# Output projection with four whole token blocks, three MLP pairs multiplied ahead, and the attention sink as a score column

## The chip, the cores and the metric

The kernel runs on one core of a Trainium2 chip. Its engines are TensorE (PE, with its weight loads as PEld), VectorE (DVE), ScalarE (ACT), GpSimd (POOL) and SyncE (SP), which issues the DMA transfers. The metric is the device time of one launch in microseconds (us), median of several runs; lower is better.

## The reference

A trunk of two layers works on 1024 tokens of 1024 features (float32). Layer 0 mixes tokens by two recurrences (RG-LRU and HGRN2 head groups side by side), layer 1 by windowed attention; each mixer ends in an output projection, a norm and a residual addition, and is followed by a squared-ReLU MLP (1024 to 4096 to 1024) with norms before and after it.

```python
for layer in range(DEPTH):
    un = rmsnorm(h, g[0])
    m = rec_mixer(un, ...) if layer % 2 == 0 else window_attention(un, ...)   # each ends in @ w_out / @ w_o
    h = h + rmsnorm(m, g[1])
    m = sqrelu_mlp(rmsnorm(h, g[2]), mlp_w1[layer], mlp_w2[layer])   # square(relu(u @ w1)) @ w2
    h = h + rmsnorm(m, g[3])
```

Attention has 16 query heads in 4 groups; a block of 128 queries sees its own key block and one on either side. Each head has a sink logit that enters the softmax as one more score and is then dropped:

```python
sc = jnp.where(band_mask, einsum(q, k) * HEAD_DIM ** -0.5, -inf)
p = softmax(concatenate([sc, sink], axis=-1), axis=-1)[..., :-1]
o = einsum(p, v)
```

## The kernel before

Every large product is made from three TensorE products of operands cut into a high and a low part (`split`, lines 84 to 86: ACT copies the high part, DVE subtracts it to get the low part), so a block of output costs three matmuls for each 128 rows of contraction. The kernel is written as a sequence of calls; a scheduler orders each engine's instructions by that sequence and by buffers and inputs being free. Two strings, `REC_ORDER` and `ATT_ORDER`, give the order of steps inside the two mixers; `!` marks a step with raised priority. In `REC_ORDER`, `G` is a gate slab (48 matmuls of 512 columns, then a sigmoid), `S` and `s` the forward and backward stage of a head, `O` its end. Every engine executes its list in order. SP holds nearly all DMA issues.

**Attention** (`unit`, line 1140). A unit is one head group and one query block: four heads. For each head PE makes the scores in PSUM (lines 1150, 1151), and DVE adds the mask, writes them to a tile `sm` and keeps the row maximum in one column of `mx` (line 1153). After the fourth head DVE makes the negative maximum `nm` against the sink (1157) and `es` = sink minus maximum (1159); ACT takes its exponential (1160) and the exponentials of the four score tiles with their sums `den` (1163). DVE adds `es` to `den` (1164), inverts it (1165), scales the four tiles (1167); PE turns them (1172), ACT and DVE split them (1175), PE multiplies by the values (1177, 1178) and DVE adds the halves into `ys` (1183). POOL multiplies and adds the rotary terms and makes low parts (1078, 1079, 1106, 86) for the projections that run between the units.

**Output projection** (`out_proj`, line 252). The contraction has eight slices of 128; slices 4 to 7 belong to the mixer's later heads. A first pass multiplies slices 0 to 3 for all eight token blocks, 192 matmuls, and ACT copies the sums away (273), four blocks into `acc`, four into tiles `ax` that DMAs bring over later (282). It can run while the mixer still works on slices 4 to 7. Then the pool `op` opens, the other slices are split, the first two weight slabs of the MLP are loaded and split (`prefetch`, 284), and a second pass multiplies slices 4 to 7 for all blocks, another 192 matmuls, which DVE adds to `acc` (288). After each block `add_norm` (231) multiplies by the norm's weight on POOL (236), normalises, adds the residual (238), stores it and normalises again for the MLP (185). Blocks 0 to 3 are turned on PE in this pass (`turn`), two products behind.

**First MLP product** (`strassen_in`, line 310). Sixteen pairs of 128 hidden columns are each computed with seven products of 12 matmuls (a Strassen scheme) in place of eight. Products 1 and 2 need only token blocks 0 to 3; the others need blocks 4 to 7, turned by `turn_far` (401). Two pairs (`lead`) have products 1 and 2 done first; their other products come in the order 6, 7, 5, 4, 3, interleaved between the pairs. The activation operands are made by bulk subtractions and splits of 128x2048 (504, 506, 512, 517, 519), and the weight operands by `lead_sums`, `sum_op` and `half`. From the third pair on the loop at line 531 repeats. `mlp`'s second product follows.

Of the kernel before, what the change touches and what calls it, by code (L numbers as in the profile page):

```python
# [18 lines left out]
P = 128  # L19
# [20 lines left out]
             "Z2 G2 S2 z2 s2 G3 !O2 z3 V3 Q3 S3 s3 O3")  # L40
# [11 lines left out]
def trunk_kernel(ctx, tc, x, norm_g, rec_w_in, rec_conv_w, rec_conv_b, rg_w_r, rg_b_r, rg_w_i,  # L52
# [199 lines left out]
    def out_proj(ys, w, h_src, h_dst, layer, nxt, pre):  # L252
# [9 lines left out]

        for k in range(4):
            two(k)
        acc = [yp.tile([P, D], F32, tag="y", name=f"acc{b}") for b in range(4)]
        far = []
        for i in range(2):
            t = xp.tile([P, 2, S], F32, tag="x", name=f"ax{i}")
            far += [t[:, b, :] for b in range(2)]
        ws = [load_wo(k, wp, "w1", 3) for k in range(3)] + [load_wo(3, xp, "x", 8)]  # L270
        for b in range(NB):
            dst = acc[b] if b < 4 else far[b - 4]
            g2_block(b, [hid[k] for k in range(4)], ws, lambda sl, o: A.activation(dst[:, sl], o, AF.Copy))
        with phase("op") as pool:
# [12 lines left out]
            def evac(sl, o):  # L287
                return V.tensor_tensor(acc[b][:, sl], o, acc[b][:, sl], op=ALU.add)
# [17 lines left out]
    def mlp(xt, hgs, layer, h_src, h_dst, nxt, pre):  # L306
# [3 lines left out]
        def strassen_in(pool):  # L310
# [4 lines left out]
            def load(p):  # L315
                if p == 1:
                    t = [yp.tile([P, KT, P], F32, tag="y", name="rawy") for _ in range(2)]
                    for e in range(2):
                        c0 = (2 * p + e) * P
                        Y.dma_start(t[e], w1[:, c0:c0 + P].rearrange("(k p) c -> p k c", p=P))  # L320
                    raws[p] = t
                else:
                    if p == 0:
                        t = wp.tile([P, KT, 2 * P], F32, tag="w1", name="raw0", bufs=3)
                    else:
                        t = xp.tile([P, KT, 2 * P], F32, tag="x", name="raw2")
                    Y.dma_start(t, w1[:, 2 * p * P:2 * (p + 1) * P].rearrange("(k p) c -> p k c", p=P))
                    raws[p] = [t[:, :, 0:P], t[:, :, P:2 * P]]
# [48 lines left out]
            def prep_step(p, slot):  # L377
# [4 lines left out]
                elif slot == 3:  # L382
                    sums2(p)
                    if (p, 1) not in ops:
                        half(p, 0, 1, 2)
# [10 lines left out]
            def act_tiles(i):  # L396
                acts[i] = tuple(pool.tile([P, 4, 512], F32R, name=f"x{v}_{i}") for v in "hl")
# [3 lines left out]
            def turn_far(b):  # L401

                blk = block_cols(b)
                (h3, l3), (h6, l6) = ((t[:, :, blk] for t in acts[i]) for i in (3, 6))
# [3 lines left out]
                V.tensor_tensor(t2[:, :, blk], p4, t1[:, :, blk], op=ALU.subtract)  # L408
                A.activation(h3, p4, AF.Copy)
                V.tensor_tensor(l3, p4, h3, op=ALU.subtract)  # L410
                split(h6, l6, t2[:, :, blk])
# [28 lines left out]

            def rest(p, slot):
# [20 lines left out]
                elif slot == 6:  # L462
# [4 lines left out]
                    if p not in place:  # L467
                        for h in (1, 0):
                            Y.dma_start(hid_d[2 * p + h], outs[p][h])
                        return  # L470
                    ch, n = place[p]
                    a11, a21, a12, a22 = c(0, 0), c(0, 1), c(1, 0), c(1, 1)
                    s1, s2, s4 = u2, u3, yp.tile([P, 512], F32, tag="y", name="s4")
# [27 lines left out]
            for p in range(lead):  # L501
                rest(p, 1)
# [798 lines left out]
```

## Time and profile before

| | |
|---|---|
| median of 3 runs (lowest to highest) | 2274.64 us (2272.72 to 2275.80) |
| the profiled execution's own time | 2273.52 us |
| its span, first to last instruction | 2271.8 us |
| PE busy | 2174.1 us, 96% |
| DVE busy | 1728.0 us, 76% |
| ACT busy | 1145.0 us, 50% |
| POOL busy | 223.1 us, 10% |
| mean granted TensorE clock | 0.984 |

The profiled execution lies 1.12 us under the median. PE's share is an average: in the two MLPs PE never pauses, and all its idle time lies in the mixers, the output projections and the starts of the MLPs.

### The profile page before, as it was taken

The page shows a single profiled execution, that of the slowest core. Times are in us where ns is not written, and L with a number is a line of the kernel's source. Part 1 is how long each engine was busy: PE and PEld are TensorE (multiplying, and loading weights), DVE is VectorE, ACT ScalarE, POOL GpSimd, SP SyncE. Part 2 cuts the span into 40 slices and gives each one's busy share as a digit, 9 for nine tenths or more (in the row PEclk, how much of TensorE's full clock was granted, in tenths as well). Part 3 has the DMA queues.
Part 4 walks back from the last instruction along what each step waited for, and adds up shares of the span by engine and source line. Part 5 has one row for each costly group of instructions (what it writes and reads, how often), then busy time and mean ns, then how long its engine had stood idle before and what let it go on. Part 6 is the DMA issues. An engine that isn't in the chain of part 4 may idle for free. (4 is left out here: it accounts for less than half of the span.)

```text
span 2271.8 us, 28186 instructions
## 1 busy us (share of the span) xinstructions
PE 2174.1 (96%) x10392; PEld 1790.7 (79%) x10392; DVE 1728.0 (76%) x2941; ACT 1145.0 (50%) x1812; POOL 223.1 (10%) x128
## 2 busy tenths in 40 slices
PE   8999999998899999999999888989899999999998
PEld 8878888887788888888878666767678888888886
DVE  6697767758866665778887888997986666578887
ACT  6566445544544456333344665765554445533342
POOL 0230000003000000000022244211200000000003
PEclk9999999999999999999999999999999999999999
DMA  5111011143444446444344112114334443744433
GB/s 148 53 33 56 29 29 30 46 139 121 135 153 153 151 141 255 145 152 153 114 148 125 33 38 56 33 33 152 132 135 153 153 153 136 245 138 153 153 118 129
DMA packets 180764, 264.03 MB, mean 116 GB/s; under 512 B 17041, under 2 KB 98961, under 8 KB 180625
## 3 DMA queue, kind: packets, MB, share of 16 engines
q1 hardware_dynamic: 180624, 262.22, 35.2%
q8 instruction: 82, 1.34, 0.3%
q14 instruction: 58, 0.47, 0.1%
HBM read 179.87 MB, written 70.78 MB: 110 GB/s over the span
## 5 line engine op out<-in xcount | busy, mean ns | idle before, releaser
L116 PE MATMUL m<-xh,w1hl 128*128 128x512 f32 (+1 forms) x1472 | 431.8, 372 | 0.0
L116 PEld LDWEIGHTS m<-xh,w1hl 128*128 128x128 f32 x1472 | 268.9, 193 | 38.1 <-ACT xh L204 0.2
L116 PE MATMUL m<-xl,w1hl 128*128 128x512 f32 (+1 forms) x736 | 274.1, 373 | 0.5 <-DVE xl L205 0.5
L236 POOL TENSOR_TENSOR mg<-acc,g 128x1024 f32<-128x1024 f32 x32 | 82.5, 2577 | 1695.1 <-DVE acc L553 1210.8
L86 DVE TENSOR_TENSOR w1hl<-raw,w1hl 128x1024 fp32r<-128x1024 f32 x108 | 135.9, 1259 | 107.0 <-ACT w1hl L85 106.9
L418 PE MATMUL aux<-xh,w1hl 128*128 128x512 f32 x512 | 169.0, 392 | 0.0
L418 PE MATMUL m<-xh,w1hl 128*128 128x512 f32 x512 | 168.0, 390 | 0.0
L418 PE MATMUL m<-xh,ws 128*128 128x512 f32 x512 | 167.8, 389 | 0.0
L567 ACT ACTIVATE hidh<-hidl 128x1536 fp32r<-128x1536 f32 (+1 forms) x56 | 89.5, 1598 | 145.1 <-DMA hidl<-hs 145.1
L644 PE MATMUL m<-w2h,hidh 128*128 128x512 f32 x416 | 161.8, 389 | 0.0
L644 PE MATMUL m<-w2l,hidh 128*128 128x512 f32 x416 | 161.8, 389 | 0.0
L644 PE MATMUL m<-w2h,hidl 128*128 128x512 f32 x416 | 161.8, 389 | 0.0
L116 PEld LDWEIGHTS m<-xl,w1hl 128*128 128x128 f32 x736 | 142.3, 193 | 19.7 <-DVE xl L205 0.8
L568 DVE TENSOR_TENSOR hidl<-hidl,hidh 128x1536 fp32r<-128x1536 f32 (+1 forms) x56 | 105.9, 1891 | 54.4 <-ACT hidh L567 54.4
L85 ACT ACTIVATE w1hl<-raw 128x1024 fp32r<-128x1024 f32 x116 | 122.4, 1056 | 40.7 <-DMA raw<-in_mlp_w_dram 21.3
L85 ACT ACTIVATE w2h<-b 128x1536 fp32r<-128x1536 f32 (+1 forms) x48 | 76.7, 1599 | 103.7 <-PE m L644 60.6
L85 ACT ACTIVATE ws<-s 128x512 fp32r<-128x512 f32 x88 | 55.7, 634 | 144.6 <-PE m L418 87.2
L644 PE MATMUL aux<-w2h,hidh 128*128 128x512 f32 x312 | 121.4, 389 | 0.0
L644 PE MATMUL aux<-w2l,hidh 128*128 128x512 f32 x312 | 121.4, 389 | 0.0
L644 PE MATMUL aux<-w2h,hidl 128*128 128x512 f32 x312 | 121.4, 389 | 0.0
L418 PEld LDWEIGHTS aux<-xh,w1hl 128*128 128x128 f32 x512 | 96.6, 189 | 20.3 <-ACT u L434 0.4
L418 PEld LDWEIGHTS m<-xh,w1hl 128*128 128x128 f32 x512 | 96.2, 188 | 20.3 <-ACT xh L85 0.4
(298 smaller groups left out, 5152.9 us busy)
## 6 DMA issues: line engine op xcount, KB each, us to landing
hidl<-hs SPq DMA_DIRECT2D x42, 768.0 KB, 4.5
raw<-in_mlp_w_dram SPq DMA_DIRECT2D x30, 1024.0 KB, 5.5
hs<-hid SPq DMA_DIRECT2D x104, 256.0 KB, 2.1
b<-in_mlp_w_dram SPq DMA_DIRECT2D x24, 768.0 KB, 4.8
raw<-in_rec_w_in_dram SPq DMA_DIRECT2D x28, 512.0 KB, 3.7
hidl<-hs SPq DMA_DIRECT2D x14, 1024.0 KB, 5.6
hs<-u SPq DMA_DIRECT2D x52, 256.0 KB, 2.0
hres<-hb SPq DMA_DIRECT2D x24, 512.0 KB, 2.7
```

Of the source, the lines that this page charges most:

```text
L85: A.activation(hi, src, AF.Copy)
L86: (eng or V).tensor_tensor(lo, src, hi, op=ALU.subtract)
L116: T.matmul(o[:, c0:c0 + nw], a[:, k, :], b[k // 4][half][:, k % 4, c0:c0 + nw], start=(n == 0), stop=(n == 3 * KT - 1))
L236: G.tensor_tensor(mg, m, g_post, op=ALU.mult)
L418: T.matmul(o, a[:, k, :], b[:, k, :], start=(first and n == 0), stop=(n == 11), skip_group_check=not first)
L567: A.activation(h, f32(l), AF.Copy)
L568: V.tensor_tensor(l, f32(l), h, op=ALU.subtract)
L644: T.matmul(o, a_[:, j, sl], b_[:, j, :], start=(not more and n == 0), stop=(n == last), skip_group_check=more)
```

## The change

In `unit`, the four score tiles become one tile with 385 columns for each head. POOL writes the negated sink into column 0. The masked scores are scaled by -0.125 as they are written behind it, and the running extreme is a minimum that starts from the negated sink (a per-partition operand in place of a constant), so it is `nm` itself. The exponential runs over the sink's column and the scores, so the sum has the sink in it. `mx`, `es` and three small DVE operations and one of ACT go.

In `out_proj`, the first pass covers token blocks 4 to 7 alone (96 matmuls). Blocks 0 to 3 are multiplied whole, eight slices, in the second pass, which ACT copies away; blocks 4 to 7 get their second half there, added by DVE. The tiles `ax` and their DMAs go. The prefetch of MLP slabs moves behind block 3 and brings three slabs; the turning of blocks 0 to 3 moves behind blocks 4 to 6.

In `strassen_in`, three pairs have products 1 and 2 done first. Two of them go on with products 3, 5, 6, 7, 4, each for both pairs side by side, as their operands come; each product's operand is split in bulk. The raw weights of pairs 0 and 1 are loaded, 1024 KB each, into tiles of the MLP's own pool. In `REC_ORDER` step G3 moves from before O2 to behind S3.

```diff
-             "Z2 G2 S2 z2 s2 G3 !O2 z3 V3 Q3 S3 s3 O3")
+             "Z2 G2 S2 z2 s2 !O2 z3 V3 Q3 S3 G3 s3 O3")
...
-        for b in range(NB):
-            dst = acc[b] if b < 4 else far[b - 4]
-            g2_block(b, [hid[k] for k in range(4)], ws, lambda sl, o: A.activation(dst[:, sl], o, AF.Copy))
+        for b in range(4, NB):
+            g2_block(b, [hid[k] for k in range(4)], ws, copy)
...
-            for b in range(4, NB):
-                acc.append(yp.tile([P, D], F32, tag="y", name=f"acc{b}"))
-                Y.dma_start(acc[b], far[b - 4])
-            ws = [load_wo(k, pool, "wo", 4) for k in range(4, KT)]
-            prefetch(pre)
+            ws += [load_wo(k, pool, "wo", 4) for k in range(4, KT)]
...
             for b in range(NB):
-                ins = g2_block(b, [hid[k] for k in range(4, KT)], ws, evac)
+                if b < 4:
+                    ins = g2_block(b, [hid[k] for k in range(KT)], ws, copy)
+                else:
+                    ins = g2_block(b, [hid[k] for k in range(4, KT)], ws[4:], add)
                 if b >= 1:
                     add_norm(b - 1, ins)
-                if 2 <= b < 6:
-                    turn(b - 2)
+                if b == 3:
+                    prefetch(pre)
+                if b == 4:
+                    turn(0)
+                if 4 <= b < 7:
+                    turn(b - 3)
...
+                if p < 2:
+                    t = pool.tile([P, KT, 2 * P], F32, tag="x" + "hl"[p] + "_7", name="raw2")
                 else:
+                    t = xp.tile([P, KT, 2 * P], F32, tag="x", name="raw2")
+                Y.dma_start(t, w1[:, 2 * p * P:2 * (p + 1) * P].rearrange("(k p) c -> p k c", p=P))
...
+            def side_by_side(p, i):
...
+                product(o, p, i, i != 4, True)
+                if i == 3:
+                    A.activation(c(0, 1), o, AF.Copy)
+                elif i == 5:
+                    outs[p].append(yp.tile([P, S], F32, tag="y", name="hid1"))
+                    A.activation(c(1, 1), o, AF.Copy)
+                    V.tensor_tensor(c(0, 1), o, c(0, 1), op=ALU.add)
+                elif i == 6:
+                    V.tensor_tensor(u2, o, u2, op=ALU.add)
+                    V.tensor_tensor(c(0, 1), c(0, 1), u2, op=ALU.add)
+                    relu2(p, 0, 1, None)
+                elif i == 7:
+                    V.tensor_tensor(u3, o, u2, op=ALU.add)
+                    V.tensor_tensor(c(1, 1), c(1, 1), u3, op=ALU.add)
+                    relu2(p, 1, 1, None)
+                else:
+                    V.tensor_tensor(c(1, 0), o, u2, op=ALU.add)
+                    relu2(p, 1, 0, None)
+                    store(p)
...
-            lead = 2
+            lead, both = 3, (0, 1)
             for p in range(lead):
                 pre_a(p)
-            load(0)
+            for p in both:
+                load(p)
             lead_sums(0)
+            sum_op(0, 3)
...
             p1(0)
+            p1(1)
             turn_far(4)
-            p1(1)
+            p2(0)
             turn_far(5)
-            p2(0)
...
+            p2(1)
             turn_far(6)
-            p2(1)
+            lead_sums(1)
+            sum_op(1, 3)
+            p1(2)
             turn_far(7)
...
+            p2(2)
+            for p in both:
+                side_by_side(p, 3)
...
-                    s_ = pool.tile([P, nk * P], F32, tag="sm", name="sm", bufs=8)
-                    V.tensor_tensor_reduce(out=s_, in0=o, in1=mask[:, mo:mo + nk * P], scale=1.0, scalar=-1e30,
-                                           op0=ALU.add, op1=ALU.max, accum_out=mx[:, j:j + 1])
-                    sm.append(s_)
-                nm = pool.tile([P, GRP], F32, tag="nm", name="nm", bufs=2)
-                V.scalar_tensor_tensor(nm, mx, -0.125, nsink[:, g * GRP:(g + 1) * GRP], op0=ALU.mult, op1=ALU.min)
-                es = pool.tile([P, GRP], F32, tag="es", name="es", bufs=1)
-                V.tensor_tensor(es, sink[:, g * GRP:(g + 1) * GRP], nm, op=ALU.add)
-                A.activation(es, es, AF.Exp)
+                sm = pool.tile([P, GRP, 3 * P + 1], F32, tag="sm", name="sm", bufs=2)
+                G.tensor_copy(sm[:, :, 0:1], nsink[:, heads].rearrange("p (j o) -> p j o", o=1))
...
+                    V.tensor_tensor_reduce(out=sm[:, j, 1:1 + nk * P], in0=o, in1=mask[:, mo:mo + nk * P], scale=-0.125,
+                                           scalar=nsink[:, g * GRP + j:g * GRP + j + 1], op0=ALU.add, op1=ALU.min,
+                                           accum_out=nm[:, j:j + 1])
                 for j in range(GRP):
-                    A.activation(sm[j], sm[j], AF.Exp, scale=0.125, bias=nm[:, j:j + 1], accum_out=den[:, j:j + 1])
-                V.tensor_tensor(den, den, es, op=ALU.add)
+                    e_ = sm[:, j, 0:1 + nk * P]
+                    A.activation(e_, e_, AF.Exp, scale=-1.0, bias=nm[:, j:j + 1], accum_out=den[:, j:j + 1])
...
-                           [(mlp_w1[layer], 2 * j * P) for j in range(2)])
+                           [(mlp_w1[layer], 2 * j * P) for j in range(3)])
```

In the rest of the lead, not shown, each of products 5, 6 and 7 is preceded by a bulk split of its activation operand and by the weight operands of both pairs; the old function `rest` keeps its order for the third pair and all later ones.

More of the change, by code (lines that the diff above doesn't have):

```diff
@@ L261, in load_wo, with copy, add @@
             return load_split(w[k * P:(k + 1) * P, :], [P, D], pool, tag, bufs)
+        def copy(sl, o):
+            return A.activation(acc[b][:, sl], o, AF.Copy)
+        def add(sl, o):
+            return V.tensor_tensor(acc[b][:, sl], o, acc[b][:, sl], op=ALU.add)
         for k in range(4):
             two(k)
[L265 to L269, printed above, removed]
+        acc = {b: yp.tile([P, D], F32, tag="y", name=f"acc{b}") for b in range(4, NB)}
         ws = [load_wo(k, wp, "w1", 3) for k in range(3)] + [load_wo(3, xp, "x", 8)]
[L271 to L273 removed]
+        for b in range(4, NB):
+            g2_block(b, [hid[k] for k in range(4)], ws, copy)
         with phase("op") as pool:
@@ L383, in prep_step @@
                     sums2(p)
-                    if (p, 1) not in ops:
+                    if p >= lead:
                         half(p, 0, 1, 2)
@@ L396, in act_tiles @@
             def act_tiles(i):
-                acts[i] = tuple(pool.tile([P, 4, 512], F32R, name=f"x{v}_{i}") for v in "hl")
+                acts[i] = tuple(pool.tile([P, 4, 512], F32R, tag=f"x{v}_{i}", name=f"x{v}_{i}") for v in "hl")
             b11, b21 = xt.f[0][0], xt.f[1][0]
@@ L466, in rest @@
                     relu2(p, 0, 1, None)
[L467 to L473, printed above, removed]
-                    V.tensor_tensor(s1, a21, a22, op=ALU.add)
-                    V.tensor_tensor(s2, s1, a11, op=ALU.subtract)
@@ L500, in strassen_in @@
-            sum_op(1, 6)
-            for p in range(lead):
-                rest(p, 1)
-            half(0, 1, 7, 4)
+            p2(2)
+            for p in both:
+                side_by_side(p, 3)
+            act_tiles(5)
+            split(*acts[5], t1)
+            for p in both:
+                sum_op(p, 5)
+            for p in both:
+                side_by_side(p, 5)
+            act_tiles(6)
+            split(*acts[6], t2)
+            for p in both:
+                sum_op(p, 6)
@@ L504, in strassen_in @@
             V.tensor_tensor(b11, t2, b11, op=ALU.subtract)
+            for p in both:
+                half(p, 1, 7, 4)
+            for p in both:
+                side_by_side(p, 6)
             act_tiles(7)
             split(*acts[7], b11)
-            half(1, 1, 7, 4)
-            for p in range(lead):
-                rest(p, 3)
-            sum_op(0, 5)
-            act_tiles(5)
-            split(*acts[5], t1)
-            sum_op(1, 5)
-            for p in range(lead):
-                rest(p, 4)
@@ L516, in strassen_in @@
-            load(2)
             V.tensor_tensor(b21, b21, t2, op=ALU.subtract)
+            for p in both:
+                side_by_side(p, 7)
             acts[4] = x_tile("xh_4"), x_tile("xl_4")
             split(*acts[4], b21)
-            sum_op(0, 3)
-            for p in range(lead):
-                rest(p, 5)
-                prep_step(2, 2 + p)
-            sum_op(1, 3)
+            load(2)
+            prep_step(2, 2)
+            prep_step(2, 3)
+            side_by_side(0, 4)
+            prep_step(2, 4)
@@ L525, in strassen_in @@
             load(3)
-            rest(0, 6)
-            prep_step(2, 4)
-            rest(1, 6)
+            side_by_side(1, 4)
             prep_step(2, 5)
             prep_step(2, 6)
-            for p in range(lead, n_pair):
-                p1(p)
+            for p in range(2, n_pair):
+                if p >= lead:
+                    p1(p)
                 if 4 <= p + 2 < n_pair:
```

67 lines of the change are left out of this document (35 added, 32 removed).

## Prediction

> **What bounds the kernel now.** I read the page first, then the busy time by stage, then who PE waited for, then single stretches. The page:
>
> ```profile
> span 2271.8 us, 28186 instructions
> PE 2174.1 (96%) x10392; PEld 1790.7 (79%) x10392; DVE 1728.0 (76%) x2941; ACT 1145.0 (50%) x1812; POOL 223.1 (10%) x128
> ```
>
> PE bounds the whole, so only time in which PE stands, or runs at a lower clock, can be won. The stages (columns: length, then PE, PEld, DVE, ACT, POOL busy with counts, granted clock, DMA) are the last recurrent head, layer 0's output projection with the MLP's start, a piece of the MLP, the attention units, and layer 1's output projection with the MLP's start:
>
> ```profile
> 434.00:482.00 48.00, 47.45 (x311) 39.48 (x310) 27.36 (x68) 17.50 (x33) 0.00 (x0) 1.00 0.07 23
> 605.00:850.00 245.00, 245.00 (x1083) 202.93 (x1082) 168.75 (x238) 124.17 (x186) 0.00 (x0) 1.00 0.45 155
> ...
> 482.00:605.00 123.00, 109.11 (x482) 88.15 (x481) 102.66 (x166) 66.55 (x115) 22.84 (x8) 0.94 0.43 147
> 1235.00:1554.00 319.00, 285.96 (x1394) 223.12 (x1395) 277.45 (x776) 204.00 (x497) 93.50 (x63) 0.96 0.14 39
> 1554.00:1672.00 118.00, 100.47 (x438) 80.27 (x437) 102.30 (x159) 62.24 (x109) 21.33 (x8) 0.93 0.43 145
> ```
>
> In the MLP PE never stands: 245 us / 1083 = 0.226 us a matmul, nothing to win. In the other three DVE is as full as PE: 102.66 of 123, 277.45 of 319, 102.30 of 118 us. Who PE waited for says the same:
>
> ```profile
> PE aux L1172 <- DVE sm L1167: 12.5, 13, 1.9
> PE aux L418 <- ACT xh L85: 9.6, 2, 4.9
> PE aux L191 <- DVE acc L185: 9.6, 6, 3.9
> ...
> PE aux L1178 <- DVE pl L86: 6.0, 8, 1.7
> ```
>
> Transposes in attention wait for DVE's scaled scores, the MLP's lead for its far operand, the turning for the norms.
>
> **Part 1, attention: three DVE operations and one of ACT fewer.** The groups of the attention stage, by engine and shape:
>
> ```profile
> L1157 DVE SCALAR_TENSOR_TENSOR nm<-mx,nsink 128x4 f32<-128x4 f32 x32 | 9.8, 310 | 0.3
> L1159 DVE TENSOR_TENSOR es<-sink,nm 128x4 f32<-128x4 f32 x32 | 10.5, 328 | 0.3
> L1164 DVE TENSOR_TENSOR den<-den,es 128x4 f32<-128x4 f32 x32 | 10.2, 319 | 11.9 <-ACT sm L1163 11.4 <-ACT es L1160 0.3
> L1167 DVE TENSOR_SCALAR sm<-sm,den 128x384 f32<-128x384 f32 x96 | 48.1, 550 | 0.4
> L1163 ACT ACTIVATE sm<-sm,nm 128x384 f32<-128x384 f32 x96 | 58.1, 608 | 22.2 <-DVE nm L1157 21.9
> ```
>
> Three go: 9.8 + 10.5 + 10.2 = 30.5 us of busy time. That is the ceiling, since the mean of 0.31 to 0.33 us is not the usual duration:
>
> ```profile
> 1339.81 0.15 DVE L1157 SCALAR_TENSOR_TENSOR nm<-mx,nsink 128x4 f32<-128x4 f32 x1
> 1339.88 0.68 DVE L1077 TENSOR_TENSOR qf<-qf,cos 128x512 f32<-128x512 f32 x1
> ...
> 1361.29 5.54 DVE L1167 TENSOR_SCALAR sm<-sm,den 128x384 f32<-128x384 f32 x4
> ...
> 1361.37 2.81 POOL L1106 TENSOR_TENSOR qst<-qf,qst 64x512 fp32r<-64x512 f32 x2 [1.79 <-ACT qst L1105]
> 1364.27 2.35 POOL L86 TENSOR_TENSOR w1hl<-raw,w1hl 128x1024 fp32r<-128x1024 f32 x1
> ```
>
> Undisturbed the operation takes 0.15 us, and the next one starts 0.07 us after it. Where POOL works, DVE operations that read SBUF alone stand: four scalings last 5.54 us, about as long as POOL's three operations of the same moment (5.2), against 4 x 0.55 = 2.2 at their mean. So of the 30.5 us, 96 x 0.15 = 14.4 are the operations' own and 16.1 are waiting for POOL. The floor is the issue distance, 96 x 0.07 = 6.7. I take 96 x 0.10 = 9.6 and half of the waiting, 8.0, because the next such operation, a scaling, inherits the rest: 17.6 us.
>
> The Trainium skill, SBUF — State Buffer, "Who interferes with whom", has the rule behind this: VectorE and GpSimd take one pair of ports in turn, each for a whole instruction. The 5.54 us row agrees. It speaks against the added POOL copies, which by it each block such a DVE operation for their length. Were every copy to meet one, at the 0.5 us of the row below, attention would win 18 - 13 = 5 us and the time be 2260 by that rule, against 2247 by the share that I take from the rows.
>
> Added: 32 POOL copies of 128x4 and, in the 128 score operations, a per-partition operand for a constant. Neither stands in the trace; the nearest rows are POOL's mask operation, and two DVE operations of equal size with and without such an operand:
>
> ```profile
> L1061 POOL TENSOR_SCALAR_AFFINE_SELECT mask<-mask 128x384 bf16<-128x384 bf16 x1 | 0.5, 507 | 0.1
> ...
> 519.36 1.28 DVE L238 SCALAR_TENSOR_TENSOR hb<-mg,r,hb 128x1024 f32<-128x1024 f32 x1
> ...
> 491.79 1.23 DVE L86 TENSOR_TENSOR wohl<-raw,wohl 128x1024 fp32r<-128x1024 f32 x1 [1.60 <-ACT wohl L85]
> ```
>
> A copy costs 0 to 0.5 us of POOL, 0 to 16 in all; DVE stands for a copy only when it is in a scaling or a rotary operation, about a fifth of the stage ((48.1 + some 15) / 319), so I take 3. The operand costs 0 to 0.05 x 128 = 6.4; I take 3. The extra column (385 for 384) and the one-column shift I cost at nothing: the ACT groups show 608 ns for 384 columns, a 384th of which is 1.6 ns, hidden by ACT's half-empty queue.
>
> The order inside a unit gets shorter as well. ACT waited 21.9 us for `nm` and DVE 11.4 for the exponentials. Now each head's exponential can start behind its own score operation, not behind the fourth and two more. Of the 11.4 I take 7. Attention: 17.6 - 3 - 3 + 7 = **18 us** (bounds: 30.5 + 11.4 = 42 gained, and 6.7 - 16 - 6.4 = 16 lost). DVE is the fuller engine there, so a microsecond of it counts nearly in full.
>
> **Part 2, output projection.** 96 of 192 first-pass matmuls (21.7 us) leave the time before the mixer's end and come behind it. First the junction: how far PE is covered from the mixer's last write until the last weight slice is split. The last `ys` write and the last split of both layers, and the first-pass matmuls in the mixers' ends (their PE and PEld columns):
>
> ```profile
> 481.73 0.75 DVE L1005 SCALAR_TENSOR_TENSOR y<-aux,ng,y 128x512 f32<-128x512 f32 x1 [0.81 <-PE aux L1003]
> ...
> 494.92 1.22 DVE L86 TENSOR_TENSOR wohl<-raw,wohl 128x1024 fp32r<-128x1024 f32 x1
> ...
> 1552.84 1.17 DVE L1183 TENSOR_TENSOR y<-aux,posb 64x128 f32<-64x128 f32 x4 [1.28 <-ACT posb L1180]
> ...
> 1566.91 1.23 DVE L86 TENSOR_TENSOR wohl<-raw,wohl 128x1024 fp32r<-128x1024 f32 x1 [0.20 <-ACT wohl L85]
> ...
> 434.00:482.00 48.00, 28.32 (x113) 20.42 (x114) 1.00 0.07 23
> 1485.00:1554.00 69.00, 37.62 (x126) 23.49 (x127) 0.98 0.07 24
> ```
>
> Both take 14 us (494.92 + 1.22 - 481.73 - 0.75 = 13.7; 1566.91 + 1.23 - 1552.84 - 1.17 = 14.1), bridged today by the 192 - 113 = 79 and 192 - 126 = 66 matmuls that are left. Layer 0 keeps some cover: G3's 48 matmuls move into that stretch, 96 + 48 - 113 = 31 are left, 7.0 us; block 0's first 18 matmuls (slices 0 to 5, whose inputs are early) give 4.1; 14 - 11 = 3 us stand. Moving G3 changes no count, and its sigmoid now sits in front of the backward stage's exponentials on ACT, whose cover is that same 48-us stretch with ACT at 17.50; 0 to 4 us, taken 0. Layer 1 has 0 left: 14 - 4 = 10, of which I take 8, since the splits need not all come last (bounds 0 and 12).
>
> Then the blocks. These rows are PE's stands in the second pass, at the start of the MLP (product 1 begins, the first far product begins) and one set of eight transposes:
>
> ```profile
> 522.57 1.27 PE L191 MATMUL aux<-ident,acc 128*128 128x128 f32 x8 [3.66 <-DVE m L148]
> ...
> 557.10 0.39 PE L418 MATMUL aux<-xh,w1hl 128*128 128x512 f32 x1
> ...
> 578.67 0.79 PE L418 MATMUL aux<-xh,ws 128*128 128x512 f32 x1 [4.69 <-ACT xh L85]
> ...
> 1623.10 0.39 PE L418 MATMUL aux<-xh,w1hl 128*128 128x512 f32 x1
> ...
> 1649.19 0.79 PE L418 MATMUL aux<-xh,ws 128*128 128x512 f32 x1 [4.93 <-ACT xh L85]
> ...
> 559.83 1.03 PE L191 MATMUL aux<-ident,acc 128*128 128x128 f32 x8
> ```
>
> With 0.226 a matmul and 0.13 a transpose (1.03 / 8), 482 to 605 holds 418 x 0.226 + 64 x 0.13 = 102.8 us of work and loses 20.2; 1554 to 1672 holds 374 x 0.226 + 8.3 = 92.8 and loses 25.2. These are what parts 2 and 3 can win, less what they lose anew. DVE's prices:
>
> ```profile
> L288 DVE TENSOR_TENSOR acc<-m,acc 128x512 f32<-128x512 f32 x16 | 10.9, 684 | 0.2 <-PE m L216 0.2
> ...
> L185 DVE SCALAR_TENSOR_TENSOR acc<-hb,r,g 128x1024 f32<-128x1024 f32 x8 | 12.5, 1560 | 0.0
> L238 DVE SCALAR_TENSOR_TENSOR hb<-mg,r,hb 128x1024 f32<-128x1024 f32 x8 | 12.4, 1552 | 0.4
> ...
> L504 DVE TENSOR_TENSOR xf<-t,xf 128x2048 f32<-128x2048 f32 x1 | 2.3, 2292 | 0.0
> ```
>
> Half the additions go: 8 x 0.68 = 5.5 us of DVE a layer; ACT's copies stay 16. An `add_norm` is (12.5 + 12.4) / 8 = 3.1 plus eight small operations of 0.15 or more, 4.5 in all. In blocks 0 to 3 PE has 4 x 48 x 0.226 = 43.4 us, DVE three norms, 13.5: no stand. In blocks 4 to 7 PE has 21.7 + 4.2 for turning; DVE must do eight additions 5.5, eight turning subtractions 5.5, three slab splits 3.7 and norm 3, 4.5, together 19.2: it fits, 1 us lost. The prefetch's three DMAs and their ACT copies lie under the same 26 us.
>
> **Part 3, start of the MLP.** Today 557.10 to 578.67 holds 48 matmuls and 32 transposes, 15.0 us, and loses 6.6; in layer 1 it loses 11.1. Afterwards 72 matmuls lie there. From the end of block 3 to the first far product PE has 21.7 + 4.2 + 16.3 + 4.2 = 46.4 us; DVE has five norms 22.5, additions 5.5, turning 5.5, slabs 3.7, far turning 9 x 0.68 = 6.1, weight sums 3.4, together 46.7. Level, so 3 us lost. Behind it come four products for two pairs, 96 x 0.226 = 21.7 us of PE, against DVE's four splits and two subtractions of 2.29, two halves 2.5, sums 6.1 and evacuations 4.1, together 26.4: 5 lost, 7 with a lower clock after each stand. The raw loads of pairs 0 and 1 now wait for the projection pool's tiles and stand behind the last norm's loads and store on SP; both have some 20 us until they are used, cost 0 to 6, taken 1.
>
> New losses: layer 0, 3 + 1 + 3 + 7 + 1 = 15 against 20.2; layer 1, 8 + 1 + 3 + 7 + 1 = 20 against 25.2. **Gain 5 and 5 us.**
>
> **Sum.** 18 + 5 + 5 = 28. Against the profiled execution, 2273.5 - 28 = 2245.5; the median is 1.1 above that execution, so 2246.6, say **2247 us**.
>
> **The rivals.**
>
> *More.* The POOL waits go with their operations and nothing inherits them (attention 26), and the junctions stay bridged because the scheduler puts slices 0 to 3 of several blocks there (another 9 and 3): 28 + 8 + 12 = 48, 2227 us. For it: POOL is busy only 93.50 of 319. Against: 5.54 us lost by scalings, which stay.
>
> *Attention alone.* Moving 21.7 us of matmuls behind the mixers wins nothing: junctions of 10 and 6, late raw loads of 4: gain 18 - 2, 2259 us. For it: the same 14 us in both layers. Against: losses of 20.2 and 25.2 leave room.
>
> *Slower: POOL's queue holds the scores.* The copy of a unit stands behind whatever POOL does in order, and the exponentials wait for it; behind it in turn wait rotary terms and low parts, and for those the next projections. At 1361 three POOL operations follow each other for 5.2 us. A copy hit by such a row, 5.2 less the 2.5 us that four score operations take, costs 2.7; for all 32 units 86 us, for 20 of them 54. It decides from 28 / 32 = 0.9 us a unit; with 20 units, 2275 - 28 + 54 = 2301 us. For it: POOL's waits in that stage. Against: the copy needs only a free `sm` tile, which it has a unit ahead.
>
> *No change.* DVE's saved time returns as waiting for PE, ACT and POOL in a chain that stays as long: 2275 us.
>
> **How the numbers follow.** Chances: forecast 0.52, more 0.16, attention alone 0.18, slower 0.08, no change 0.06. Times under 2270.1 are faster by over 0.2% and over 2279.2 slower, about what can be told from no change: faster 0.52 + 0.16 + 0.18 = 0.86, same 0.06, slower 0.08. The forecast's own range is 2236 to 2258; with the rivals on either side, 2223 to 2267 leaves the slow case and no change out.
>
> **What would show it.** Right: the groups for `nm`, `es` and the `den` addition gone, DVE in attention down by 10 to 20 us, the exponentials' wait for `nm` much under 21.9; the mixers' ends earlier; no stand of PE in the four whole blocks; the first far product waiting under 4.69 us. Wrong: waits of ACT or DVE on POOL's `sm`, scalings far above 550 ns, a PE gap over 10 us at the junction, `lead_sums` waiting for its DMA.

## The result, and the profile after

The changed kernel takes 2244.12 us (median, 2242.00 to 2245.58), against 2274.04 us (2272.72 to 2275.80) for the kernel before: a ratio of 0.9867, 95% interval 0.9850 to 0.9884, 30 us won. The forecast was 2247, with a range of 2223 to 2267. The sum was right, 28 us for 30. Its terms were not: attention was put too high, the two other stages too low.

The totals, from the page of the changed kernel (busy time, share of the span, instructions):

```profile
span 2242.6 us, 28121 instructions
PE 2163.7 (96%) x10392; PEld 1781.4 (79%) x10392; DVE 1686.3 (75%) x2827; ACT 1145.3 (51%) x1782; POOL 229.5 (10%) x160
```

PE executes as many matmuls as before, and is busy 10.4 us less (2174.1 before). Its idle time falls by 18.8 us, from 97.7 to 78.9. So a third of the gain of 29.2 us in the span is not idle time: the same matmuls ran faster. The stages show where. I cut them at events, not at times, so that each holds the same work in both kernels as far as it can: from the mixer's last write to the end of three pairs' products (252 matmuls) in layer 0; attention from its first score matmul to its last `ys` write; and from there to the end of three pairs' products in layer 1. Busy time by stage of the kernel before (length, then PE, PEld, DVE, ACT, POOL busy with counts, granted clock, DMA share, GB/s):

```profile
482.50:629.40 146.90, 133.01 (x588) 107.94 (x587) 121.68 (x192) 80.87 (x136) 22.84 (x8) 0.95 0.47 160
1235.90:1554.00 318.10, 285.96 (x1394) 223.10 (x1395) 276.58 (x775) 204.00 (x497) 92.60 (x62) 0.96 0.14 39
1554.00:1701.20 147.20, 129.67 (x567) 104.47 (x566) 126.70 (x193) 79.84 (x135) 21.33 (x8) 0.94 0.47 159
```

The same stages of the kernel after:

```profile
480.70:617.10 136.40, 131.38 (x599) 106.15 (x598) 110.69 (x178) 80.85 (x136) 21.66 (x8) 1.00 0.44 151
1223.50:1531.50 308.00, 275.40 (x1353) 214.84 (x1354) 258.14 (x681) 202.44 (x463) 99.49 (x92) 0.97 0.15 40
1531.50:1672.10 140.60, 134.32 (x609) 107.80 (x608) 110.12 (x178) 81.46 (x137) 20.96 (x8) 1.00 0.43 146
```

Layer 0 is 10.5 us shorter. Attention is 10.1 us shorter, but with 41 matmuls fewer in it, and the stage behind it is 6.6 us shorter with 42 more; only the sum of these two, 16.7 us, can be compared. The recurrence ends 1.8 us earlier, and the rest of the MLPs is unchanged (0.2 us). That is 29.2 us.

Two things are to be seen. In attention PE stands as long as before, 318.10 - 285.96 = 32.1 and 308.00 - 275.40 = 32.6 us, although DVE has 18.4 us less to do. In the other two stages PE's standing falls from 13.9 to 5.0 and from 17.5 to 6.3 us, and the clock, 0.95 and 0.94 before, is 1.00.

Who PE waited for, in the kernel after (in all, times, longest):

```profile
PE aux L1207 <- ACT ph L85: 7.3, 12, 1.0
...
PE aux L1202 <- DVE sm L1197: 5.5, 7, 1.0
...
PE aux L191 <- DVE t L402: 3.1, 2, 1.6
PE m L413 <- ACT ws L85: 3.0, 2, 1.5
```

The 9.6 us for the first far product are gone, and the 9.6 us for `acc` are down to 0.6; what is left at the start of the MLP is, in each layer, some 1.5 us for a turned block and 1.5 us for a weight operand. In attention the transposes' wait for the scaled scores is down from 12.5 to 5.5 us, and the products' wait for `ph` up from 2.1 to 7.3: waiting changed its place there.

The groups of attention, after (busy, mean ns of one, idle before and its releasers):

```profile
L1193 ACT ACTIVATE sm<-sm,nm 128x385 f32<-128x385 f32 x96 | 58.3, 610 | 5.5 <-DVE nm L1187 3.6 <-POOL sm L1181 1.3
L1187 DVE CUSTOM_DVE_ANT_0 sm<-m,mask,nsink 128x384 f32<-128x384 f32 x96 | 56.2, 614 | 10.5 <-PE m L1186 7.4 <-PE aux L1202 1.5 <-POOL qf L1112 1.1
...
L1197 DVE TENSOR_SCALAR sm<-sm,den 128x384 f32<-128x384 f32 x96 | 45.7, 533 | 0.2
...
L1187 DVE CUSTOM_DVE_ANT_0 sm<-m,mask,nsink 128x256 f32<-128x256 f32 x32 | 14.5, 479 | 5.1 <-PE m L1186 4.4 <-PE aux L1202 0.5
...
L1181 POOL COPY sm<-nsink 128x4 f32<-128x4 f32 x30 | 8.1, 270 | 102.3 <-PE aux L1202 78.8 <-ACT ph L85 9.0 <-DVE qf L1110 7.8
L1194 DVE RECIPROCAL den<-den 128x4 f32<-128x4 f32 x32 | 5.6, 174 | 2.9 <-ACT sm L1193 2.5
```

and the score operation and the exponential before:

```profile
L1163 ACT ACTIVATE sm<-sm,nm 128x384 f32<-128x384 f32 x96 | 58.1, 608 | 22.2 <-DVE nm L1157 21.9
...
L1153 DVE CUSTOM_DVE_ANT_0 sm<-m,mask 128x384 f32<-128x384 f32 x96 | 50.7, 554 | 7.8 <-PE m L1151 3.6 <-PE aux L1172 3.1
...
L1153 DVE CUSTOM_DVE_ANT_0 sm<-m,mask 128x256 f32<-128x256 f32 x32 | 12.5, 421 | 5.2 <-PE m L1151 2.7 <-PE aux L1172 2.3
```

The per-partition operand costs 60 ns a score operation, at 384 columns (554 to 614) as at 256 (421 to 479), 7.5 us over 128. The exponentials wait 5.5 us where they waited 22.2, and the inversion waits 2.5 us for them where the `den` addition waited 11.4. POOL's copies take 8.1 us; they wait long, and 1.3 us of ACT's waiting is put down to them.

### The profile page after: what moved, and what is told of

It is laid out like the page before. It is cut to its first block, busy times and chain, and to the rows that moved or that the text cites. A ratio compares the mean times of both kernels' runs of the same rounds, so it can differ in the third digit from the quotient of the medians.

```text
span 2242.6 us, 28121 instructions
## 1 busy us (share of the span) xinstructions
PE 2163.7 (96%) x10392; PEld 1781.4 (79%) x10392; DVE 1686.3 (75%) x2827; ACT 1145.3 (51%) x1782; POOL 229.5 (10%) x160
## 4 chain that ended last, share of the span: by engine, by line
PE 74%; DVE 16%; ACT 5%; issue 2%; DMA 2%; POOL 1%; SPq 0%; DVEq 0%; ACTq 0%; POOLq 0%
PE m L413 14%; PE m L677 13%; PE m L116 12%; PE aux L677 9%; PE aux L413 9%; PE m L216 9%; DVE sm L1197 1%; PE aux L948 1%; PE aux L1202 1%; DVE hb L238 1%; DVE w1hl L86 1%; DVE acc L185 1%; PE aux L1207 1%; PE aux L1026 1%; PE aux L949 1%
## 5 line engine op out<-in xcount | busy, mean ns | idle before, releaser
L116 PEld LDWEIGHTS m<-xh,w1hl 128*128 128x128 f32 x1472 | 267.5, 193 | 38.8 <-ACT qf L1107 1.6
L601 DVE TENSOR_TENSOR hidl<-hidl,hidh 128x1536 fp32r<-128x1536 f32 (+1 forms) x56 | 105.9, 1890 | 54.5 <-ACT hidh L600 54.5
L85 ACT ACTIVATE w1hl<-raw 128x1024 fp32r<-128x1024 f32 x118 | 124.1, 1054 | 34.3 <-DMA raw<-in_mlp_w_dram 10.1
L85 ACT ACTIVATE ws<-s 128x512 fp32r<-128x512 f32 x88 | 55.4, 631 | 140.2 <-PE m L413 78.6
L413 PEld LDWEIGHTS m<-xh,ws 128*128 128x128 f32 x512 | 95.8, 188 | 28.3 <-ACT ws L85 5.5
```

The source lines that it names most:

```text
L85: A.activation(hi, src, AF.Copy)
L116: T.matmul(o[:, c0:c0 + nw], a[:, k, :], b[k // 4][half][:, k % 4, c0:c0 + nw], start=(n == 0), stop=(n == 3 * KT - 1))
L413: T.matmul(o, a[:, k, :], b[:, k, :], start=(first and n == 0), stop=(n == 11), skip_group_check=not first)
L601: V.tensor_tensor(l, f32(l), h, op=ALU.subtract)
```

## The experiments

Each kernel was timed beside the kernel before, whose median was 2273.4 to 2274.9 us each time.

**The sink alone, and all but the sink.** The new `unit` in the kernel before, and the old `unit` in the kernel after (the edit told in words):

```diff
 # e1_sink: the kernel before with
-    (mx, es, four tiles sm, three small DVE operations)
+    (one tile sm of 385 columns, G.tensor_copy of the sink, scalar=nsink[...], op1=ALU.min)
 # e2_rest: the kernel after, with the reverse of this
```

> The kernel before with the sink as score column and start value alone. The prediction's sizes: the attention units 18 us shorter, 2256 us. Rival, read from the trace after: the score operation's operand costs 7.5 us of VectorE and POOL waits at the copy, so the units win 6 to 10 us, 2264 to 2268 us. If VectorE's time came back as waiting: 2274 us.

> The changed kernel with the attention unit of before: whole blocks, three pairs ahead, products in operand order and G3 moved. The prediction's sizes: 5 us a layer, 2264 us. Rival, read from the trace after: PE hardly stands in the four whole blocks or at the first far product, 9 to 11 us a layer, 2252 to 2256 us.

The kernel before with the sink alone: 2267.3 us, ratio 0.9969 (0.9956 to 0.9982), 7.6 us won. With the rest alone: 2249.0 us, ratio 0.9885 (0.9870 to 0.9899), 25.9 us won. The first lies in its rival's range, the second 3 us under its own rival's. Together they are 33.5, against 30 for the whole; the 3.5 us between are no more than the intervals' widths, so it is not shown that anything is won only once. The forecast's 18 for attention is refuted, and so are its 10 for the two other stages.

**The two halves of the rest.** The new output projection alone (two pairs ahead, old order of products), and the new start of the MLP alone (three slabs fetched in the old projection):

```diff
 # e4_op: the kernel before with out_proj of the kernel after
 # e5_mlp: the kernel before with mlp of the kernel after, and
-                           [(mlp_w1[layer], 2 * j * P) for j in range(2)])
+                           [(mlp_w1[layer], 2 * j * P) for j in range(3)])
```

> The kernel before with the new output projection alone: four blocks whole, prefetch of two slabs behind block 3, two pairs ahead and the old order of products. If the whole blocks carry the gain (VectorE's backlog taken off while PE has 43 us): 2262 to 2266 us. If the third pair and the order carry it: 2272 to 2278 us, and PE waits 5 us or more for the first far product as before.

> The kernel before with the new start of the MLP alone: three slabs prefetched in the old output projection, three pairs ahead, products in operand order. If the third pair and the order carry the gain (5.4 us more cover, first far product after 72 matmuls): 2262 to 2266 us. If the whole blocks carry it: 2270 to 2276 us, because VectorE still comes to the far turning with the old backlog.

2261.4 us, ratio 0.9937 (0.9913 to 0.9962), and 2258.1 us, ratio 0.9930 (0.9915 to 0.9945): 13.6 and 16.8 us, about equal parts. Both lie under 2262 to 2266, the range that each text gave to the case that its half carries the gain, so each carries a part. Who PE waited for with the new output projection alone:

```profile
PE aux L421 <- ACT xh L85: 9.6, 2, 4.9
```

and with the new start of the MLP alone:

```profile
PE aux L191 <- DVE acc L185: 8.3, 5, 2.4
...
PE m L410 <- ACT ws L85: 4.5, 3, 2.7
```

The new projection alone leaves the first far product's 9.6 us as they were; the new start alone leaves 8.3 of the 9.6 us for `acc`, and halves the wait at the first far product. The sum of the two, 30.4, is over the 25.9 us of both together, but not by more than the intervals allow; that part of the idle time can be won by either is likely and not shown.

**Two pairs ahead, products in the new order.**

```diff
-            lead, both = 3, (0, 1)
+            lead, both = 2, (0, 1)
...
-            p1(2)
             turn_far(7)
-            p2(2)
...
-                           [(mlp_w1[layer], 2 * j * P) for j in range(3)])
+                           [(mlp_w1[layer], 2 * j * P) for j in range(2)])
```

> The kernel after with two MLP pairs ahead in place of three (the products stay in operand order; two slabs fetched in the output projection). Theory A: the third pair's two products (5.1 us of TensorE) are the cover for the last block's norm and turn, so each of the two layers loses 2 to 5 us: 2248 to 2254 us. Theory B: the order of the products gives it all, the far product's operand being ready by then: within 2 us of 2244.1.

2253.4 us, ratio 0.9911 (0.9896 to 0.9926): 9.2 us slower than the kernel after, as theory A has it. In the profiled executions layer 0's stage ends 4.1 us later (621.2 for 617.1 us from the start), and attention and layer 1's stage together are 4.0 us longer. PE's instructions at the first far product of layer 0 in this kernel (start, duration, what it waited for):

```profile
563.84 1.06 PE L191 MATMUL aux<-ident,acc 128*128 128x128 f32 x8 [0.18 <-DVE t L406]
570.40 0.79 PE L413 MATMUL m<-xh,ws 128*128 128x512 f32 x1 [5.50 <-ACT ws L85]
```

It stands 5.50 us for the weight sum, where the kernel after has the third pair's 24 matmuls (24 x 0.226 = 5.4 us). So the new order of the products alone does not remove the wait; the third pair covers most of it.

**The move of G3 in the recurrence.**

```diff
-             "Z2 G2 S2 z2 s2 !O2 z3 V3 Q3 S3 G3 s3 O3")
+             "Z2 G2 S2 z2 s2 G3 !O2 z3 V3 Q3 S3 s3 O3")
```

> The kernel after with the recurrence order of before (G3 ahead of !O2). The prediction costed this move at 0, with 0 to 4 us as bounds: by it the time stays within 2 us of 2244.1. The rival: the ends of the recurrence that lie 2 to 3 us earlier in the changed kernel (480.7 and 479.3 against 482.5 us from the start) come from the move, and in one direction: 2246 to 2248 us.

2241.1 us (2240.0 to 2242.9), ratio 0.9858 (0.9842 to 0.9874). The direction is the other way from the rival's: the old order is 3 us better, if anything, 1 us outside the prediction's 2. Three pairs' products of layer 0 end at 615.7 us from the start there, at 617.1 in the kernel after. The intervals of the two kernels overlap, so this is not settled; that the move gains nothing is.

**The operand.**

```diff
-    scalar=nsink[:, g * GRP + j:g * GRP + j + 1], op0=ALU.add, op1=ALU.min,
+    scalar=1e30, op0=ALU.add, op1=ALU.min,
```

> The kernel after with a constant (1e30) as start of the score operation's minimum in place of the per-partition operand; the sink is still a column of the scores, so the softmax is the same up to the value that is subtracted. The score operation should fall from 614 to about 554 ns (384 wide) and from 479 to 421 (256 wide), 7.5 us over 128. Theory A: attention's length follows VectorE, and 5 to 8 us of it come back: 2236 to 2239 us. Theory B: attention is now held by ScalarE and by the order on GpSimd, and VectorE's time is spare: within 2 us of 2244.1.

2248.7 us (2241.6 to 2252.2), ratio 0.9886 (0.9867 to 0.9906): not faster. The score operation in this kernel, and its attention by stage:

```profile
L1187 DVE CUSTOM_DVE_ANT_0 sm<-m,mask 128x384 f32<-128x384 f32 x96 | 50.7, 554 | 13.7 <-PE m L1186 8.6 <-PE aux L1202 4.2
```

```profile
1223.00:1530.00 307.00, 274.37 (x1324) 214.61 (x1325) 254.35 (x681) 200.95 (x460) 95.42 (x92) 0.94 0.15 41
1530.00:1676.80 146.80, 140.42 (x638) 113.25 (x637) 110.17 (x179) 82.83 (x140) 20.93 (x8) 1.00 0.42 140
```

The operand's price is gone again, 554 for 614. But attention is only 1.0 us shorter with 29 matmuls (6.6 us) fewer in it; PE stands 32.6 us once more, and the clock is 0.94 where it was 0.97 (14.5 us lost to it by windows of 5 us, against 8.6). The 5.6 us that are missing are about the 5.9 us more that went to the clock. Theory A falls. Theory B's range is missed by 2.6 us, but four runs from 2241.6 to 2252.2 do not refute it. DVE's time was saved, and nothing came of it that can be told. The same edit together with the old recurrence order:

> The kernel after with the recurrence order of before and the constant start of the score operation, the two edits that are on record one by one (2241.1 and 2248.7 us). If their effects add, 2246 us. If the 2248.7 came from where attention's stands happened to fall (the granted clock was 0.94 there, against 0.97 in after), the operand's 7.5 us of VectorE show now: 2234 to 2240 us.

2244.6 us, ratio 0.9873 (0.9859 to 0.9888), 3.5 us slower than that order without it: the two effects nearly add. Twice, then, 5.5 us saved in the wide score operations made nothing faster.

**The column written by DVE.**

```diff
-    G.tensor_copy(sm[:, :, 0:1], nsink[:, heads]...)
+    V.tensor_copy(sm[:, :, 0:1], nsink[:, heads]...)
```

> The kernel after with the sink column written by VectorE in place of GpSimd. Theory A (the copy, which waits 102 us on GpSimd for the transposes of the unit two back, holds up the low parts and rotary pieces queued behind it, and through them the score operations): 3 to 6 us faster than after, 2238 to 2241 us, though VectorE has 30 small instructions more. Theory B (GpSimd's waiting costs nothing): 30 instructions of 0.15 to 0.3 us on VectorE are paid, 2246 to 2253 us.

2244.9 us, ratio 0.9875 (0.9860 to 0.9890): no change. Theory A is refuted: nothing is won by freeing POOL's queue. Of theory B's range the lower end is missed by 1 us, so 32 more DVE instructions, 14.6 us of busy time in this row, cost nothing that can be told either (that the two effects hide each other is possible and not tested):

```profile
L1181 DVE COPY sm<-nsink 128x4 f32<-128x4 f32 x32 | 14.6, 459 | 4.2 <-PE aux L1202 4.0
```

**Three small operations put back.**

```diff
+    [V.tensor_tensor(tm, sink[:, heads], nsink[:, heads], op=ALU.add) for _ in range(3)]
```

> The kernel after with three small VectorE operations (128x4, results unused) put back in each of the 32 attention units, behind the score operations, where before had its three; they read constants and nobody waits for them. It tells apart what the sink change alone was worth (7.6 us). Theory A (it is VectorE's instruction time, as the prediction had it with 17.6 us for them): most of the 7.6 us goes again, 2249 to 2253 us. Theory B (it is the shorter order inside a unit, exponentials that need not wait for nm): within 2 us of 2244.1.

2247.5 us, ratio 0.9888 (0.9872 to 0.9905). This one does not answer its question. The operations' own view (shortest, median and longest in ns, first and last start) shows why:

```profile
L1191 DVE TENSOR_TENSOR tm<-sink,nsink x96: 146/159/2334, 1204.0 to 1227.7; 128x4 f32<-128x4 f32 x96
```

Since they read constants, the scheduler set all 96 ahead of the units, in the 24 us before attention's first scores. How much of the 7.6 us is DVE's instructions and how much the shorter order inside a unit stays open. The two edits before this one speak against DVE's instructions: 7.5 us of DVE less and 14.6 us more in the units changed the time in neither case by what they took.

**Fillers against the clock.** PE's instructions around its longest stand in the recurrence, in the kernel after, show what the clock does:

```profile
155.10 0.39 PE L116 MATMUL m<-xl,w1hl 128*128 128x512 f32 x1
161.05 2.05 PE L864 MATMUL aux<-xc,kd 128*128 128x512 f32 x4 [5.57 <-DVE xc L852]
...
165.03 0.63 PE L864 MATMUL aux<-xc,kt 128*128 128x512 f32 x1
165.46 0.63 PE L864 MATMUL aux<-xc,kd 128*128 128x512 f32 x1
...
169.41 0.39 PE L864 MATMUL aux<-xc,kt 128*128 128x512 f32 x1
169.64 0.61 PE L864 MATMUL aux<-xc,kd 128*128 128x512 f32 x2
```

Behind the stand a matmul starts every 0.43 us (165.03 to 165.46), some microseconds later every 0.23 (169.41 to 169.64). If that is lost time, matmuls that only keep PE busy should win some of it (`fill` puts a number of them in front, into a bank that is started afresh):

```diff
 # g1_fill: the kernel before, first far product of pair 0
-                    banks[p, "b"] = mm_ps("aux")
+                    banks[p, "b"] = fill(mm_ps("aux"), acts[2][0], 16 if p == 0 else 0)
 # g2_best: the kernel after with the old recurrence order, first gate product
-                    pr, pi = mm_ps("aux"), mm_ps("aux")
+                    pr, pi = fill(mm_ps("aux"), xt.h[0][0], 22 if hb == d == hf == 0 else 0), mm_ps("aux")
```

> The kernel before with 16 more matmuls (of operands that lie ready, into the bank that the far product starts afresh, so that they change nothing) in front of the first far product of each layer, where TensorE stands 4.69 and 4.93 us. They take 16 x 0.227 = 3.6 us a layer. Theory A (part of the old loss is the granted clock, which falls behind a stand and makes each matmul last 0.43 in place of 0.227 us): the fillers take idle time only, the clock stays at 1.00 behind them where it was 0.52 to 0.80 (from 575) and 0.50 to 0.84 (from 1645), and 2 us a layer come back: 2268 to 2271 us against 2274. Theory B (only the stands count): no change, 2273 to 2275 us. Theory C (the fillers push the far products back): up to 7 us slower, 2275 to 2281 us.

> The kernel after with the recurrence order of before and 22 fillers of the same kind in front of the first gate product of the recurrence, where TensorE stands 5.6 us in every kernel here and the clock then falls to 0.50. Theory A (the clock falls behind the stand): 22 x 0.227 = 5.0 us of the stand are filled, the clock stays, and 2.5 to 3 us are won on the 2241.1 us of that kernel without fillers: 2237.5 to 2239.5 us. Theory B (only stands count): 2240 to 2242 us.

The first: 2271.2 us, ratio 0.9993 (0.9984 to 1.0002), no difference that can be told. The first far product of layer 0 by windows of 5 us, before:

```profile
575.00:580.00 5.00, 0.79 (x1) 0.28 (x1) 5.00 (x9) 4.57 (x6) 0.00 (x0) 0.80 0.14 54
580.00:585.00 5.00, 4.54 (x11) 3.62 (x12) 4.41 (x5) 2.91 (x3) 0.00 (x0) 0.52 0.00 0
585.00:590.00 5.00, 4.51 (x21) 3.41 (x20) 4.72 (x5) 1.43 (x3) 0.00 (x0) 1.00 0.00 0
```

and with the fillers:

```profile
575.00:580.00 5.00, 3.16 (x13) 2.08 (x12) 5.00 (x7) 3.38 (x6) 0.00 (x0) 1.00 0.00 2
580.00:585.00 5.00, 4.95 (x21) 3.33 (x19) 5.00 (x6) 2.70 (x3) 0.00 (x0) 1.00 0.00 0
585.00:590.00 5.00, 4.08 (x18) 3.27 (x18) 5.00 (x6) 0.37 (x1) 0.00 (x0) 1.00 0.55 160
```

The clock stayed at 1.00 there, as theory A has it. From the start of the stand to the end of the stage (573.99 to 629.40 us before, 571.64 to 626.10 with the fillers) 55.4 us became 54.5: 1.0 us is won of the 2 that theory A has for a layer. The whole stage is 146.7 us, 146.9 before. DVE is full or nearly so in every row, and the products wait for it again: 1.28 us behind the first far matmul, 0.99 before. In layer 1 the clock held only until 1655 us, where it fell behind another stand of 1.96 us, and the same stretch takes 56.9 us in both kernels. So theory A is right on the clock in layer 0, and at most a quarter of its 4 us shows. The interval leaves room for up to 3.6 us; a small gain is not excluded.

The second: 2250.2 us, ratio 0.9895 (0.9882 to 0.9909), 9 us slower than without fillers, against both theories. Where the fillers ran in this kernel (shortest, median and longest in ns, first and last start), and PE's wait at the stand:

```profile
L858 PE MATMUL aux<-xh x22: 389/389/396, 78.0 to 82.8; 128*128 128x512 f32 x22
...
PE aux L864 <- DVE xc L852: 5.4, 1, 5.4
```

The fillers' operands are ready early, and all 22 run at 78.0 to 82.8 us, among dense matmuls, 77 us before the stand. The stand is as long as before, only later: DVE's instructions up to its operand are the same in the same order, and the operand is cast at 164.03 us where it was cast at 159.89. So the fillers cost their own 5 us and filled nothing; where the other 4 us went stays open. The run says nothing on the clock.

## Why the prediction was right in the sum and wrong in its terms

The sum came near by luck: attention was put 10 us too high (18 for 7.6) and the other two stages 16 us too low (10 for 25.9), and the two errors offset each other. What failed in each part follows.

PE's stand in a stage is its length less PE's busy time; the clock's loss is PE's busy time by one less the granted clock, summed over windows of 5 us. Of the whole span that loss is 24.7 us before and 12.6 after. By stage (us):

| kernel | layer 0: length, stand, clock | attention | layer 1: length, stand, clock |
|---|---|---|---|
| before | 146.9, 13.9, 5.2 | 318.1, 32.1, 9.5 | 147.2, 17.5, 5.6 |
| after | 136.4, 5.0, 0.0 | 308.0, 32.6, 8.6 | 140.6, 6.3, 0.0 |
| sink alone | 149.2, 15.1, 6.5 | 308.2, 31.1, 10.8 | 148.9, 12.8, 1.9 |
| all but the sink | 137.8, 6.0, 0.0 | 320.6, 31.3, 11.0 | 132.9, 9.0, 1.5 |
| projection alone | 142.2, 11.3, 3.2 | 317.7, 31.8, 6.6 | 139.2, 12.3, 5.3 |
| start of the MLP alone | 140.7, 9.8, 2.8 | 316.9, 30.4, 10.9 | 141.2, 12.9, 2.8 |
| constant start | 137.7, 5.8, 0.0 | 307.0, 32.6, 14.5 | 146.8, 6.4, 0.0 |
| two pairs ahead | 142.2, 9.4, 2.5 | 306.9, 31.4, 10.0 | 145.7, 10.0, 2.7 |

**Part 1, 18 us: mis-sized, 7.6 measured alone.** The account of DVE's time was good: three operations less, operand and copy added, 18.4 us less in the stage. The step that failed is the last one, that "a microsecond of it counts nearly in full". PE stands 30 to 33 us in attention in all eight rows, whether DVE has 277 or 254 us to do. What a shorter attention does is to use fewer of the matmuls that may fill it (1353 in place of 1394 in the stage), and these lie behind it as cover: with the sink alone it is the stage after attention in which PE's stand falls, from 17.5 to 12.8 us, and the clock's loss from 5.6 to 1.9. The run with the column on DVE shows the same trade: attention, with 14 us more of DVE, lasts 317.8 us there and holds 1388 matmuls, the stage behind it lasts 131.5 us with 575, and the sum, 449.3 us, is the changed kernel's 448.6 but for 0.7. So the gain came, but by another way, and it should be bounded by what stands there: in the changed kernel, whose later stage has less to cover, the medians give the sink 4.9 us (2249.0 less 2244.1). This account is read from the counts and the stands; no run holds the number of matmuls fixed. The two terms taken for unseen things were off as well, and nearly cancel: the operand, taken at 3 with 6.4 as its bound, is 7.5 us of DVE; the POOL copies, taken at 3, show no cost against the same copies on DVE. The earlier exponentials came as described (waits of 11.4 to 2.5 and of 22.2 to 5.5); their 7 us can't be told from the rest.

The shared ports that the Trainium skill describes (SBUF — State Buffer, "Who interferes with whom") would by the prediction's reckoning have taken 16 us for these copies, 13 more than it counted. No run shows such a loss: moving all copies from POOL to DVE left the time where it was, and the scalings take no longer in all (533 ns for 550 before at 384 columns, 476 for 456 at 256).

**Parts 2 and 3, 5 and 5 us: mis-sized, some 12 a layer measured.** With all but the sink, layer 0's stage ends 12.3 us earlier than before (617.1 for 629.4 us from the start), and attention and layer 1's stage together are 11.8 us shorter (453.5 for 465.3). The old losses were right: 20.2 and 25.2 in the prediction, 13.9 + 5.2 = 19.1 and 17.5 + 5.6 = 23.1 over somewhat longer stages here. The new losses, put at 15 and 20, are 5.0 and 6.3, with no loss to the clock. Term by term:

- *Junction, 3 and 8 us.* Nothing in layer 0, 0.97 us in layer 1. Of the 14 us between the mixer's end and the last split, 11.7 are there in layer 0 and 13.5 in layer 1. But the prediction bridged them with "block 0's first 18 matmuls"; the scheduler brings forward the early slices of more blocks. First-pass and second-pass matmuls of layer 1 up to the mixer's last write, and in the 13.5 us after it:

```profile
1228.00:1531.50 303.50, 28.63 (x93) 17.86 (x94) 0.97 0.14 39
1531.50:1545.00 13.50, 12.52 (x54) 9.33 (x52) 1.00 0.81 283
```

93 of 96 first-pass matmuls are used up, "0 left" was right to three, and 51 others come from the whole blocks in place of 18. This was the rival's reason ("slices 0 to 3 of several blocks").

- *Whole blocks, no stand; blocks 4 to 7, 1 us.* As predicted: no row of PE waiting from 480 to 548 us.
- *Before the first far product, 3 us; behind it, 7 us.* PE's waits in the changed kernel's layer 0, from 555 to 585 us, all of them:

```profile
556.38 0.50 PE L413 MATMUL aux<-xh,w1hl 128*128 128x512 f32 x1 [0.65 <-ACT u L429]
560.94 0.66 PE L191 MATMUL aux<-ident,acc 128*128 128x128 f32 x4 [1.54 <-DVE t L402]
565.86 0.47 PE L413 MATMUL aux<-xh,w1hl 128*128 128x512 f32 x1 [0.18 <-DVE t L406]
573.67 0.73 PE L413 MATMUL m<-xh,ws 128*128 128x512 f32 x2 [0.20 <-DVE ws L86]
577.74 0.50 PE L413 MATMUL m<-xh,ws 128*128 128x512 f32 x1 [1.51 <-ACT ws L85]
579.88 0.73 PE L413 MATMUL m<-xh,ws 128*128 128x512 f32 x2 [0.36 <-DVE ws L86]
```

2.4 us before (3 was right), 2.1 us behind. The 7 was the difference of two lists, 26.4 us of DVE against 21.7 of PE, and 2 for the clock. No stand here is over 1.6 us, and the clock does not fall. Without the third pair the stand is 5.50 us, and the clock falls behind it.

**The rivals.** "More", 2227, had the right reason for the junction, but its 8 us in attention are absent. "Attention alone", 2259, is refuted by the 25.9 us that the rest wins without the sink. The slower case, POOL's queue holding the scores, is refuted by the column on DVE and by 1.3 us of ACT's waiting. "No change" is refuted by the result. The move of G3, taken at 0, gains nothing and may cost 3.

**Open.** Why PE's stand in attention stays at 32 us whatever DVE has to do; and how far the lower clock costs time by itself. With 12.1 us less of it in the changed kernel it goes with the gain, but with the fillers, where DVE sets the pace, a clock that was kept up won 1.0 us in one layer and nothing in the other. The new projection and the new start of the MLP are several edits each; beyond the third pair and G3 they were not taken apart.

## What to carry to other kernels

Where independent matmuls fill a stage's gaps, a faster stage need not show a shorter stand of PE: here it gave back such matmuls, and its gain was what they covered next, so cost it there, and compare only the sum of the two stages. Time that a saturated second engine needs at a boundary (here norms and splits at the start of the MLP) can be covered with whole independent products put ahead of it; one pair more was worth 4 to 5 us a layer, nearly what its matmuls last (5.4). Fillers without use won at most 1 us where the other engine set the pace, even where they kept the clock up, and a filler whose operands are ready early can run far from the gap that it is meant for.

## What the runs showed of the hardware

A [128, 1] operand in place of a constant as the start of the fused add-and-extreme operation on DVE costs 60 ns at both widths here (554 to 614 ns at 384 columns, 421 to 479 at 256); back with the constant it is 554 again.

PE's clock can fall behind short stands. In the kernel after it fell behind one of 2.18 us; the second set of eight transposes behind it takes 1.91 us, 1.03 undisturbed:

```profile
1194.32 0.40 PE L116 MATMUL m<-xh,w1hl 128*128 128x256 f32 x2
1196.90 1.06 PE L191 MATMUL aux<-ident,acc 128*128 128x128 f32 x8 [2.18 <-DVE r L152]
...
1198.34 1.91 PE L191 MATMUL aux<-ident,acc 128*128 128x128 f32 x8
```

But the length of the stand does not decide alone. The same stand, 2.18 to 2.20 us at 1193 to 1209 us, is in all fourteen traces; the clock fell behind it in nine and stayed at 1.00 in five. The 5 us from its end, in the kernel after and with all but the sink (the clock is the third number from the right):

```profile
1196.90:1201.90 5.00, 5.00 (x30) 4.99 (x31) 4.12 (x6) 2.77 (x5) 1.01 (x2) 0.66 0.50 165
...
1196.80:1201.80 5.00, 4.98 (x42) 4.86 (x43) 4.02 (x6) 3.15 (x6) 1.02 (x2) 1.00 0.48 146
```

A stand of 1.02 us at about 220 us, also in all fourteen, was followed by a fall in three of them. In the kernel after, three stands of 1.03, 0.95 and 0.88 us within 4 us, at 1365, did it (the fall came during the third), while single ones up to 1.55 us left the clock at 1.00. Each time the clock is 0.50 for 3.41, 6.83 or 10.24 us (apart from the end of the span). So a microsecond or two in the clock's column of the table can be chance. The Trainium skill, TensorE: Matmul & The Clock Gate, "Part 1: The HAM clock gate", also has a full and a half clock, but gives an idle window of some 3.4 us as what brings the half one; the rows here show falls behind shorter stands.

A DVE operation of 128x4 takes 0.159 us in the median, and up to 2.33 us (the three put back). A copy of 128x4 is 265 to 270 ns in the mean on POOL and 459 ns on DVE.
